# A decoder block's output projection as seven block products instead of eight

## The chip, the cores and the metric

One core of a Trainium2 chip runs the kernel. The time is device microseconds of one execution, as the median of several runs. The core has five engines that run side by side, each through its own instructions in order: TensorE (PE: matmuls; its weight loads, PEld, overlap them), VectorE (DVE), ScalarE (ACT), GpSimd (POOL) and SyncE (SP, which here only issues DMAs). An instruction waits on semaphores for what it reads, and everything behind it on its engine waits with it.

## The reference

One decoder block, all in float32, for 512 tokens of 1024 channels. What matters here is the middle:

```python
merged = (sigmoid(g_attn) * (attn @ w_branch_attn)
          + sigmoid(g_pool) * (pool @ w_branch_pool))   # 512 x 1024
x = x + gate1 * (merged @ w_out)                        # w_out 1024 x 1024
h2 = rms_norm(x, norm2_g) * (1 + scale2) + shift2
u = causal_dwconv(h2 @ w_up, conv_w, conv_b)            # w_up 1024 x 5632
x = x + gate2 * ((silu(u_g) * u_v) @ w_down)            # w_down 2816 x 1024
```

Ahead of it stand an RMS norm, the input projection, attention of 8 heads with a bias by distance, and a pooling branch. The six vectors shift1, scale1, gate1, shift2, scale2, gate2 are `silu(c) @ ada_w + ada_b`, cut in six parts (numbered 0 to 5 in the kernel).

## The kernel before

**Number format.** TensorE multiplies in a reduced format (float32r). Each operand is therefore split into a high part (a copy, `_h` or `hi_`, on ACT) and a low part (operand minus high part, `_l` or `lo_`, on DVE or POOL), and every product is three matmuls: high·high, high·low, low·high (`mm3`, `more`, lines 133 to 135 and 139 to 141). A matmul contracts 128 rows and writes 128 x 512 float32, one PSUM bank. There are eight banks.

**Stages, in order of time.** Input projections P, Q, K, V (up to about 106 us); eight attention heads with the gate projections between them (106 to 226); eight blocks j of the branch projections (226 to 270); the output projection with residual and second norm (270 to 323); the up projection (315 to 550, its convolution to 555); the down projection (550 to the end). The last two are done already as products of sums of blocks: the eight products of 2 x 2 blocks are replaced by seven, of sums `s1` to `s4` on one side and `t1` to `t4` on the other. For the down projection the weights' sums are made by POOL's DMAs: `t_step` loads a block, adds another with an adding DMA, stores the sum to DRAM (`tsum`), and SP loads it again later. No two steps of one tile follow each other without waiting for the DMA to land.

**Order.** The schedule is written by hand: each engine does its instructions in the order in which the Python code issues them.

**Names.** `plan` lists the weight units that SP loads, `ahead(name, n)` loads and splits n units beyond the named one. `ada_col(g, k)` loads a 512 KB block and sums it on DVE (line 207, `raw_ada`) into one column of `acol`: block k of vector g. `row_of(g)` turns eight columns into a row across all partitions by three DMAs of POOL (`g_d`, `g`). `bias_rows(h)` issues POOL's DMA of head h's bias (`trev`), which line 603 adds to the logits. In the branch loop, `gate` tiles become the merged block j (channels 128 j on the partitions, 512 tokens along), `mg_h` and `mg_l` are its parts, and the eight 1024-wide blocks of w_out (`raw_wo`) are split by ACT and POOL (`wo_h`, `wo_l`). Then `out_mm(t, f, ..)` makes 128 tokens t of half f of the channels: 8 k x 3 matmuls into a bank `o`. `out_post` multiplies by gate1 (`g`) and adds to `x`; `out_norm` squares and sums (ACT and DVE), takes the power -1/2 on POOL (`rs_y`), scales (`xn`) and stores x to DRAM (`x2d`). `flip_h2` transposes `xn` on TensorE (`hT`), and ACT and DVE make `h2f`, `h2h`, `h2l`, which the up projection reads (`u`). In the down stage `b` are blocks of w_down, `a` and `s` blocks and sums of the activations, X, Y, Z the accumulating banks.

**Where the ada sums stood.** Of the eight blocks of vector 5 (gate2), six are summed in the Q, K and V stages, block 6 in the output projection, block 7 behind the second transposes. Of vector 4 (scale2), blocks 0 and 1 are summed in heads 6 and 7, and six blocks in the output projection.

## Time and profile before

| | |
|---|---|
| three runs, us | 661.79, 661.38, 661.92 (median 661.79) |
| profiled execution, us | 661.57, its span 659.8, granted clock 0.998 |
| output projection on TensorE | 270.16 to 315.49 us |
| second transposes on TensorE | 321.24 to 322.91 us |
| ada sums on DVE | 48, 60.6 us in all, mean 1277 ns |
| weights from HBM, whole span | 120.90 MB read, 15.76 MB written |

The profile is one execution of the program. It has busy times by engine, the chain of work that ended last, groups of instructions by line and tile, and rows of a timeline. A row of the timeline reads: start in us, duration in us, engine, line, operation, written tile, operands and shape, number of instructions, and in brackets how long the engine stood idle before it and for whom. DMA rows by tile end with the size and the median time from issue to landing in us.

### The profile page before, as it was taken

Reading aid. Unit: us, or ns where it says so; the run is one execution under the profiler, and the core shown is the slowest. Engines: PE = TensorE matmul, PEld = TensorE weight load, DVE = VectorE, ACT = ScalarE, POOL = GpSimd, SP = SyncE. Lnnn points to the kernel's source line nnn. Section 1 sums busy time; section 2 is a strip of 40 time slices with the busy share of each in tenths; the row PEclk is TensorE's granted clock in tenths of the full one; section 3 lists DMA queues with packets and bytes.
Section 4 is the critical chain, followed back from the end, with each engine's and each line's share of the span. In section 5 each row is a group of like instructions: output and inputs, shape, how many; then the busy total and the mean of one; then the engine's idle time right before and its main releaser. Section 6 shows DMA issues by size and latency. Waiting matters only on the chain.

```text
span 659.8 us, 9672 instructions
## 1 busy us (share of the span) xinstructions
PE 652.9 (99%) x3493; PEld 562.8 (85%) x3493; DVE 546.5 (83%) x932; ACT 374.0 (57%) x651; POOL 146.2 (22%) x195
## 2 busy tenths in 40 slices
PE   8999999999999999999999999999999999999997
PEld 6788788888888888888998899998999988888886
DVE  6997897788878878847679799998999797878774
ACT  8555346756664566403756566665756655768431
POOL 3003050000000046613434444444532000000000
PEclk9999999999999999999999999999999999999999
DMA  8897353255552686764599999999996343655761
GB/s 347 317 311 271 98 191 113 69 183 184 171 176 97 214 193 223 234 254 153 169 206 239 272 257 275 258 308 275 266 268 227 118 143 95 231 190 187 270 216 55
DMA packets 43365, 137.29 MB, mean 208 GB/s; under 512 B 5699, under 2 KB 6380, under 8 KB 43318
## 3 DMA queue, kind: packets, MB, share of 16 engines
q1 hardware_dynamic: 28646, 98.23, 43.7%
q0 software_dynamic: 14672, 38.45, 22.9%
q8 instruction: 27, 0.44, 0.3%
q14 instruction: 20, 0.16, 0.1%
HBM read 120.90 MB, written 15.76 MB: 207 GB/s over the span
## 4 chain that ended last, share of the span: by engine, by line
PE 96%; DMA 1%; DVE 1%; SPq 0%; ACT 0%; issue 0%
PE u L133 7%; PE u L134 7%; PE u L135 7%; PE gate_ps L133 4%; PE gate_ps L134 4%; PE gate_ps L135 4%; PE X L140 3%; PE X L139 3%; PE X L141 3%; PE uX L139 3%; PE uX L141 3%; PE uX L140 3%; PE o L135 2%; PE o L133 2%; PE o L134 2%; PE q L149 2%
## 5 line engine op out<-in xcount | busy, mean ns | idle before, releaser
L133 PE MATMUL u<-h2h,hi_up 128*128 128x512 f32 (+1 forms) x224 | 80.5, 359 | 0.0
L134 PE MATMUL u<-h2l,hi_up 128*128 128x512 f32 (+1 forms) x224 | 80.4, 359 | 0.0
L135 PE MATMUL u<-h2h,lo_up 128*128 128x512 f32 (+1 forms) x224 | 80.4, 359 | 0.0
L207 DVE CUSTOM_DVE_ANT_0 raw_ada<-raw_ada,cbc,pk 128x1024 f32<-128x1024 f32 x48 | 60.6, 1277 | 0.0
L133 PE MATMUL gate_ps<-h_h,hi_gate 128*128 128x512 f32 x128 | 50.1, 391 | 0.0
L134 PE MATMUL gate_ps<-h_l,hi_gate 128*128 128x512 f32 x128 | 50.0, 390 | 0.0
L135 PE MATMUL gate_ps<-h_h,lo_gate 128*128 128x512 f32 x128 | 50.0, 390 | 0.0
L135 PEld LDWEIGHTS u<-h2h,lo_up 128*128 128x128 f32 x224 | 42.3, 189 | 6.3
L133 PEld LDWEIGHTS u<-h2h,hi_up 128*128 128x128 f32 x224 | 42.3, 189 | 6.0
L134 PEld LDWEIGHTS u<-h2l,hi_up 128*128 128x128 f32 x224 | 42.3, 189 | 6.0
L765 POOL DMA_DIRECT2D ta<-in_wdn x33 | 29.5, 900 | 26.8 <-DMA tsum_t<-ta 17.8
L124 DVE TENSOR_TENSOR lo_t<-raw_t,hi_t 128x1024 fp32r<-128x1024 f32 (+1 forms) x24 | 26.6, 1130 | 8.9 <-ACT hi_t L114 8.9
L114 ACT ACTIVATE hi_t<-raw_t 128x1024 fp32r<-128x1024 f32 (+1 forms) x24 | 23.7, 987 | 17.2 <-PE Y L141 8.1
L766 POOL DMA_DIRECT2D tsum_t<-ta x33 | 18.5, 560 | 52.9 <-DMA ta<-in_wdn 51.1
L607 ACT ACTIVATE L<-L,mn 128x512 f32<-128x512 f32 (+3 forms) x32 | 17.6, 552 | 20.1 <-DVE mn L603 20.1
L135 PEld LDWEIGHTS gate_ps<-h_h,lo_gate 128*128 128x128 f32 x128 | 24.0, 188 | 5.1
L133 PEld LDWEIGHTS gate_ps<-h_h,hi_gate 128*128 128x128 f32 x128 | 24.0, 188 | 4.8 <-DVE mn L603 0.3
L220 POOL TENSOR_TENSOR wo_l<-raw_wo,wo_h 128x512 fp32r<-128x512 f32 x16 | 24.0, 1521 | 18.1 <-ACT wo_h L219 18.1
L134 PEld LDWEIGHTS gate_ps<-h_l,hi_gate 128*128 128x128 f32 x128 | 24.0, 188 | 4.5
L114 ACT ACTIVATE hi_up<-raw_up 128x1024 fp32r<-128x1024 f32 x24 | 25.0, 1049 | 4.3 <-PE u L134 4.3
L1250 POOL DMA_DIRECT2D x2r<-x2d x8 | 4.6, 574 | 93.5 <-DVE dt L1243 88.8
L133 PE MATMUL o<-wo_h,mg_h 128*128 128x512 f32 x64 | 25.0, 391 | 0.0
(357 smaller groups left out, 2114.7 us busy)
## 6 DMA issues: line engine op xcount, KB each, us to landing
raw_ada<-in_ada SPq DMA_DIRECT2D x48, 512.0 KB, 5.0
raw_up<-in_wup SPq DMA_DIRECT2D x44, 512.0 KB, 5.8
ta<-in_wdn POOLq DMA_DIRECT2D x44, 256.0 KB, 6.4
raw_t<-tsum_t SPq DMA_DIRECT2D x20, 512.0 KB, 3.9
tsum_t<-ta POOLq DMA_DIRECT2D x33, 256.0 KB, 5.0
raw_gate<-in_wch SPq DMA_DIRECT2D x16, 512.0 KB, 4.0
raw_b<-in_wdn SPq DMA_DIRECT2D x15, 512.0 KB, 4.2
tc<-in_wdn POOLq DMA_DIRECT2D x22, 256.0 KB, 6.2
```

The costliest lines, as they stand in the source:

```text
L114: nc.scalar.activation(hi, raw, AF.Copy)
L124: nc.vector.tensor_sub(lo, raw, hi.bitcast(F32))
L133: nc.tensor.matmul(ps, sh, mh, start=start, stop=False)
L134: nc.tensor.matmul(ps, sh, ml, start=False, stop=False)
L135: nc.tensor.matmul(ps, sl, mh, start=False, stop=stop)
L139: nc.tensor.matmul(ps, sh, mh, start=start, stop=False, skip_group_check=True)
L140: nc.tensor.matmul(ps, sh, ml, start=False, stop=False, skip_group_check=True)
L141: nc.tensor.matmul(ps, sl, mh, start=False, stop=stop, skip_group_check=True)
L207: nc.vector.tensor_tensor_reduce(out=raw, in0=raw, in1=cbc, op0=ALU.mult, op1=ALU.add, scale=1.0, scalar=col(C_AB + i), accum_out=acol[:, ...
L220: (eng or nc.vector).tensor_sub(lo[:, :w], src, hi[:, :w].bitcast(F32))
L765: add = lambda to, nm: nc.gpsimd.dma_start(to, wdn[plain[nm], i][:, us], accum_op=ALU.add)
L766: store = lambda nm, t: nc.gpsimd.dma_start(tsum[nm, i][:, us], t)
```

## The change

The output projection becomes seven products of 2 x 2 blocks. On the side of the merged activations (a11: channels 0 to 511 of tokens 0 to 255, a12: channels 512 to 1023 of the same tokens; a21 and a22 the same for tokens 256 to 511) DVE makes four sums of blocks, `gs1` to `gs4`. On the side of the weights (512 x 512 blocks b11, b12, b21, b22) POOL's DMAs make t1 to t4 during the attention heads (`out_sums`, by the same `t_step`) and store them to DRAM (`osum`). The products are a11·b11 (into banks X), a12·b21 (Z), s1·t1 (Y), s2·t2 (X), s4·b22 (Y), s3·t3 (X), a22·t4 (X), 24 matmuls of 128 x 512 each; X goes on accumulating through four of them, and ACT copies a bank's state out where it is needed in between (`ok`). The rest of the diff:

- The loop over the branch blocks splits `br` units up to two ahead and not beyond the last; the first two up units are split in the output projection.
- The low parts of b11, b21, t1, t2 are made by POOL, of b22 and t4 by DVE. Those of t3 go another way: ACT copies the high part and negates the raw block in place, four adding DMAs of POOL add the high part to it, ACT negates the result (`o_high`, `o_low`).
- The reads of banks X after s3·t3 (`o_add(2 + p, 1, "X", ..)`) stand ahead of the norms of tokens 0 to 255. a22·t4 goes into the same banks.
- `bias_rows` is issued three heads ahead instead of two.
- Vector 4's blocks 0 to 5 are summed where vector 5's were (Q, K and V stages) and 6 and 7 in the last heads. Vector 5's eight: one in the up loop behind unit 3, three before the last convolution of the up stage, one in the first product of the down stage, three in the second.

The core of the diff:

```diff
-        def t_step(kk, n):
+        def t_step(kk, n, src, dst, hold):
...
+        def out_sums(h):
+            for n in range(h % 4 * 2, h % 4 * 2 + 2):
+                for kk in range(h // 4 * 2, h // 4 * 2 + 2):
+                    if n < 7:
+                        t_step(kk, n, osrc, osum, bias[0])
...
-            if h + 2 < H:
-                bias_rows(h + 2)
+            if h + 3 < H:
+                bias_rows(h + 3)
+            out_sums(h)
...
+        def o_high(nm):
+            res = []
+            for i in range(2):
+                raw = load_unit(osrc(nm, i), f"wo_{nm}_{i}")
+                for s in range(2):
+                    hi = slot(f"wo_{nm}_{2 * i + s}_h", F32R)
+                    nc.scalar.activation(hi, raw[:, s * 512 : s * 512 + 512], AF.Copy)
+                    res.append((hi, raw[:, s * 512 : s * 512 + 512]))
+                nc.scalar.activation(raw, raw, AF.Copy, scale=-1.0)
+            for hi, r in res:
+                nc.gpsimd.dma_start(r, hi.bitcast(F32), accum_op=ALU.add)
+            return res
+        def o_low(nm, res):
+            for k, (hi, r) in enumerate(res):
+                lo = slot(f"wo_{nm}_{k}_l", F32R)
+                nc.scalar.activation(lo, r, AF.Copy, scale=-1.0)
+                wo[nm, k] = hi, lo
+        o_prod("a11", "b11", "X", by_k=True)
+        o_fetch(0, 0)
+        g_sum("s1")
+        low()
+        g_hi("s1")
+        g_sum("s2")
+        g_lo("s1")
+        o_keep("s1", "X")
+        g_hi("s2")
+        g_sum("s3")
+        g_lo("s2")
+        g_sum("s4")
+        o_prod("a12", "b21", "Z", by_k=True)
+        g_hi("s4")
+        g_lo("s4")
+        for i in range(2):
+            o_split("b22", i)
+        o_prod("s1", "t1", "Y")
+        for p in range(2):
+            o_res(p, 0, o_add(p, 0, "Z", plus="s1"))
+        o_fetch(0, 1)
+        ahead("up0", 1)
+        o_keep("s5", "Y")
+        g_hi("s3")
+        g_lo("s3")
+        t3 = o_high("t3")
+        for p in range(2):
+            o_square(p, 0)
+        o_prod("s2", "t2", "X")
+        o_keep("s2", "X")
+        o_fetch(1, 1)
+        for i in range(2):
+            o_split("t4", i)
+        o_low("t3", t3)
+        o_prod("s4", "b22", "Y")
+        for p in range(2):
+            o_res(p, 1, o_add(p, 1, "Y", minus=(None, "s2")))
+            o_square(p, 1)
+        for p in range(2):
+            o_root(p)
+        o_fetch(1, 0)
+        o_prod("s3", "t3", "X")
+        tail = []
+        for p in range(2):
+            tail.append(o_add(2 + p, 1, "X", minus=("s5", None)))
+            o_norm(p)
+        o_prod("a22", "t4", "X", (0,), range(2))
+        tps = turn_h2(1)
+        o_prod("a22", "t4", "X", (0,), range(2, 4))
+        o_prod("a22", "t4", "X", (1,))
+        for p in range(2):
+            o_res(2 + p, 1, tail[p])
+        def first_half():
+            o_res(2, 0, oacc["X", 0], slot("ot_2_0"))
+        take_h2(1, tps, {3: first_half, 5: lambda: o_square(2, 1, True), 6: lambda: o_square(3, 1, True)})
+        o_res(3, 0, oacc["X", 1], slot("ot_3_0"))
+        for p in range(2):
+            o_square(2 + p, 0)
+            o_root(2 + p)
+        for p in range(2):
+            o_norm(2 + p)
...
+                if j == 3:
+                    ada_col(5, 0)
...
+        for k in range(1, 4):
+            ada_col(5, k)
         behind(0)
         behind(1)
```

How instructions stand at three places. First DVE behind the last block of the branch loop, where the output projection begins. Before (the three gate operations of the last block, the merged block's low part, then ada sums; `acol 128x1` reads the sum out):

```order
446 L853 TENSOR_TENSOR gate_2482<-gate_2482,B_2858 128x512
447 L854 TENSOR_TENSOR gate_1855<-gate_1855,A_2871 128x512
448 L855 TENSOR_TENSOR gate_2482<-gate_2482,gate_1855 128x512
449 L220 TENSOR_TENSOR mg_l<-gate_2482,mg_h 128x512
450 L207 ISA raw_ada_2901,acol<-raw_ada_2901,cbc,pk 128x1024
451 L207 ISA acol 128x1
```

Of the changed kernel, the same place (`gs` are the block sums; the gate tiles on the right are merged blocks):

```order
446 L884 TENSOR_TENSOR gate_2542<-gate_2542,gate_1893 128x512
447 L892 SCALAR_TENSOR_TENSOR acol<-acol,pk 128x8
448 L938 TENSOR_TENSOR gs_0_2991<-gate_1929,gate_2289 128x256
449 L938 TENSOR_TENSOR gs_0_2991<-gate_2073,gate_2418 128x256
450 L938 TENSOR_TENSOR gs_1_2994<-gate_2109,gate_2454 128x256
451 L938 TENSOR_TENSOR gs_1_2994<-gate_2256,gate_2542 128x256
452 L867 TENSOR_TENSOR mgl_2942<-gate_2542,mgh_2941 128x512
```

The ada sums have left the place, and the sums and low parts of the merged blocks follow the last gate addition directly.

Second POOL in the output projection of the changed kernel: fetches of x, stores of x2d, the four adding DMAs for t3 (`raw_wo_t`, line 1045) and the powers of the first two norms.

```order
103 L1045 DMA raw_wo_t_0_3152<-wo_t_0_h 128x512
104 L1045 DMA raw_wo_t_0_3152<-wo_t_1_h 128x512
105 L987 DMA x_2_1_3204<-in_x 128x512
106 L987 DMA x_3_1_3206<-in_x 128x512
107 L1045 DMA raw_wo_t_1_3159<-wo_t_2_h 128x512
108 L1045 DMA raw_wo_t_1_3159<-wo_t_3_h 128x512
109 L1032 DMA x2d_1_3316<-x_0_1_3124 128x512
110 L1032 DMA x2d_1_3326<-x_1_1_3126 128x512
111 L987 DMA x_2_0_3280<-in_x 128x512
112 L987 DMA x_3_0_3282<-in_x 128x512
113 L1024 TENSOR_TENSOR rs_y_3274<-ms_y_3272,mhalf 128x1
114 L1024 TENSOR_TENSOR rs_y_3278<-ms_y_3276,mhalf 128x1
```

Before, POOL had no adding DMA here, and each norm's power stood behind the stores of its own tokens. Now the powers of two norms stand behind all these rows.

Third DVE before the last convolution of the up stage (`ug`, `uv`: the two halves of the last unit, convolved by line 1131, 963 before). Of the changed kernel:

```order
838 L1176 TENSOR_TENSOR s_4_6084<-s_4_6084,a_4_5671 128x512
839 L1177 TENSOR_TENSOR a_4_5673<-a_4_5671,a_4_5673 128x512
840 L207 ISA raw_ada_6096,acol<-raw_ada_6096,cbc,pk 128x1024
842 L207 ISA raw_ada_6099,acol<-raw_ada_6099,cbc,pk 128x1024
844 L207 ISA raw_ada_6102,acol<-raw_ada_6102,cbc,pk 128x1024
846 L1131 SCALAR_TENSOR_TENSOR ug_6105<-u_6009,pk,ug_6105 128x511
847 L1131 SCALAR_TENSOR_TENSOR uv_6107<-u_6010,pk,uv_6107 128x511
```

The rows left out read the sums out (`acol 128x1`). Before, rows 819 and 820 (`a_4`, then `ug`) followed each other; three ada sums now stand between them.

More of the change, by code (lines that the diff above doesn't have):

```diff
@@ L786, in t_step @@
                 store("t4", tb.pop(kk)[0])
+        osum = {(n, i): dpool.tile([P, D], F32, name=f"osum_{n}_{i}") for n in ("t1", "t2", "t3", "t4") for i in range(2)}
+        oat = {"b11": 0, "b12": 1, "b21": 4, "b22": 5}
+        osrc = lambda nm, i: osum[nm, i] if nm[0] == "t" else wout[oat[nm] + 2 * i]
+        def out_sums(h):
[3 more added lines that the diff above has]
+                        t_step(kk, n, osrc, osum, bias[0])
         gates = {}
@@ new lines, in g_hi, with g_lo, g_of @@
+        def g_hi(nm):
+            for q in range(2):
+                hi = slot(f"g{nm}_{q}_h", F32R)
+                nc.scalar.activation(hi, gsum[nm, q], AF.Copy)
+                gform[nm, q] = hi, slot(f"g{nm}_{q}_l", F32R)
+        def g_lo(nm):
+            for q in range(2):
+                hi, lo = gform[nm, q]
+                nc.vector.tensor_sub(lo, gsum[nm, q], hi.bitcast(F32))
+        def g_of(nm, k, p):
+            if nm == "a11" or nm[0] == "s":
+                o = k % 2 * 256 + p * P
+                src = (ah[k // 2], al[k // 2]) if nm == "a11" else gform[nm, k // 2]
+            else:
+                o = (nm == "a22") * 256 + p * P
+                src = ah[k + 4], al[k + 4]
+            return [t[:, o : o + P] for t in src]
@@ new lines, in block_kernel, with o_prod @@
+        oacc, okept, ofresh = {}, {}, set()
+        def o_prod(an, bn, acc, ps=(0, 1), ks=range(4), by_k=False):
+            for p, k in ([(p, k) for k in ks for p in ps] if by_k else [(p, k) for p in ps for k in ks]):
+                if (acc, p) not in oacc:
+                    oacc[acc, p] = bank(f"o{acc}_{p}")
+                a, w = g_of(an, k, p), wo[bn, k]
+                more(oacc[acc, p], a[0], a[1], w[0], w[1], (acc, p) not in ofresh, k == 3)
+                ofresh.add((acc, p))
@@ L906, in out_post, with o_square @@
             nc.vector.tensor_mul(tmp, ps, g1[f])
-            between()
             nc.vector.tensor_add(xr[t, f], xr[t, f], tmp)
-        def out_norm(t):
-            row = [xr[t, 0], xr[t, 1]]
-            rs = rms_rows(row, f"y{t}")
-            rss[4 + t] = rs
+        osq = {}
+        def o_square(t, f, on_dve=False):
+            if t not in osq:
+                osq[t] = mini.tile([P, 2], F32, tag="ss", name=f"ss_y{t}")
+            junk = slot(f"junk_y{t}_{f}")
+            if on_dve:
+                nc.vector.tensor_tensor_reduce(
+                    out=junk, in0=xr[t, f], in1=xr[t, f], op0=ALU.mult, op1=ALU.add, scale=1.0 / D,
+                    scalar=0.0, accum_out=osq[t][:, f : f + 1])
+            else:
+                nc.scalar.activation(junk, xr[t, f], AF.Square, scale=1.0 / math.sqrt(D), accum_out=osq[t][:, f : f + 1])
@@ L917, in out_norm @@
                 xn2[t, f] = n_
                 x2d[t, f] = dpool.tile([P, 512], F32, name=f"x2d_{t}_{f}")
[L919 to L939 removed]
+                nc.gpsimd.dma_start(x2d[t, f], xr[t, f])
@@ L951, in block_kernel @@
+        for p in range(2):
+            o_norm(2 + p)
         fa, forms = {}, {}
```

149 lines of the change are left out of this document (90 added, 59 removed).

## The prediction

> **What bounds the kernel now.** I read the page's head first, then who TensorE waited for, then the stage of the output projection piece by piece.
>
> ```profile
> span 659.8 us, 9672 instructions
> PE 652.9 (99%) x3493; PEld 562.8 (85%) x3493; DVE 546.5 (83%) x932; ACT 374.0 (57%) x651; POOL 146.2 (22%) x195
> PEclk9999999999999999999999999999999999999999
> PE 96%; DMA 1%; DVE 1%; SPq 0%; ACT 0%; issue 0%
> ```
>
> ```profile
> PE xT L284 <- DVE wm L164: 1.5, 1, 1.5
> PE xT L298 <- ACT x L290: 0.9, 2, 0.5
> PE uX L139 <- ACT ka L1126: 0.4, 1, 0.4
> ```
>
> The second fence is all that TensorE waited for in the whole span: 2.8 us. TensorE is the bound from end to end and its clock is granted in full in every slice. So matmuls that go come off the time one for one, and every microsecond that TensorE must newly wait goes back on. DVE has 17% idle, ACT 43%; whether that idle time lies in the right place is the question here.
>
> ```profile
> L133 PE MATMUL o<-wo_h,mg_h 128*128 128x512 f32 x64 | 25.0, 391 | 0.0
> 270.16 0.39 PE L133 MATMUL o<-wo_h,mg_h 128*128 128x512 f32 x1
> 308.25 1.92 PE L880 MATMUL hT<-pk,xn 128*128 128x128 f32 x16
> 309.92 0.47 PE L133 MATMUL o<-wo_h,mg_h 128*128 128x512 f32 x1
> 315.49 0.28 PE L133 MATMUL u<-h2h,hi_up 128*128 128x256 f32 x1
> 315.60 0.28 PE L134 MATMUL u<-h2l,hi_up 128*128 128x256 f32 x1
> 322.91 0.37 PE L133 MATMUL u<-h2h,hi_up 128*128 128x256 f32 x1
> ```
>
> The projection is 64 matmuls on each of three lines (L133 to L135, one row quoted), 192 in all, from 270.16 to 315.49, with 16 transposes inside (308.25 to 309.92, 1.67 us). So one 512-wide matmul takes (45.33 - 1.67) / 192 = 0.227 us of the stream; the 391 ns in the group row is its pipelined duration, not its price. A 256-wide one steps by 0.12 us (315.49, then about 315.6).
>
> ```profile
> 227.00:275.00 48.00, 48.00 (x214) 39.72 (x213) 38.35 (x48) 32.61 (x52) 25.80 (x19) 1.00 0.74 213
> 275.00:321.00 46.00, 46.00 (x234) 39.24 (x233) 30.08 (x61) 11.77 (x26) 12.39 (x25) 1.00 0.55 194
> ```
>
> Columns: stretch, its length, busy time (and count) of PE, its weight loads, DVE, ACT, POOL, then clock, DMA share, GB/s. In 275 to 321 DVE has 15.9 us free and ACT 34.2. The change spends them.
>
> **TensorE's gain.** Seven products of 24 matmuls are 168, so 24 fewer: 24 x 0.227 = **5.45 us** off. [...]
>
> **What must be ready, and when.** I lay the new order on the old clock, products of 24 x 0.227 = 5.45 us from 270.16: a11·b11 to 275.6, a12·b21 to 281.05, s1·t1 to 286.5, s2·t2 to 291.9, s4·b22 to 297.4, s3·t3 to 302.8, then a22·t4 with the transposes of tokens 0 and 1 inside.
>
> ```profile
> 271.47 1.14 ACT L219 ACTIVATE wo_h<-raw_wo 128x512 fp32r<-128x512 f32 x2
> 269.48 1.04 ACT L114 ACTIVATE hi_up<-raw_up 128x1024 fp32r<-128x1024 f32 x1
> 273.01 1.00 DVE L855 TENSOR_TENSOR gate<-gate,gate 128x512 f32<-128x512 f32 x1
> 275.64 1.27 DVE L207 CUSTOM_DVE_ANT_0 raw_ada<-raw_ada,cbc,pk 128x1024 f32<-128x1024 f32 x1
> 288.04 0.69 DVE L906 TENSOR_TENSOR ot<-o,g 128x512 f32<-128x512 f32 x1 [7.51 <-PE o L135]
> 288.77 0.69 DVE L908 TENSOR_TENSOR x<-x,ot 128x512 f32<-128x512 f32 x1
> 310.87 0.76 DVE L890 TENSOR_TENSOR h2l<-h2f,h2h 128x256 fp32r<-128x256 f32 x2
> ```
>
> Prices: ACT copies of 512 about 0.55, of 1024 about 0.95 (1.04 less the overlap); DVE 512-wide 0.6 in a stream and 0.72 behind the one it needs (288.04 to 288.77); 256-wide 0.35 (half of 0.76, less overlap). Over the stage DVE gets 16 block sums (16 x 0.35), 16 low parts of sums, b22 and t4 (16 x 0.6) and six more adds that read a bank (6 x 0.65), 19.1 us, and loses seven ada sums of 1.27, 8.9: 10 more into 15.9 free. In order from the last gate add (273.01 + 1.00): s1 to 275.4, the low part of the last merged block 276.0, s2 277.4, s1's low parts 278.6, s3 280.0, s2's low parts 281.2, s4 282.6, its low parts 283.8, b22's 286.2. Wanted are s1 at 281.05, s2 at 286.5, s4 and b22 at 291.9. The first five products wait for nothing; the least lead is the 2.5 us of s1, and behind it each late microsecond would be one of TensorE's.
>
> **Term 1, the low parts of t3.** They go round by ACT, POOL and a DMA: ACT copies the high part and negates the block, POOL issues an adding DMA, ACT negates the sum.
>
> ```profile
> 327.17 0.91 POOL L765 DMA_DIRECT2D ta<-in_wdn  x1 [3.09 <-DMA ta<-in_wdn]
> 333.25 0.58 POOL L766 DMA_DIRECT2D tsum_t<-ta  x1 [1.19 <-DMA ta<-in_wdn]
> ta<-in_wdn POOLq DMA_DIRECT2D x44, 256.0 KB, 6.4
> g<-g_d POOLq DMA_DIRECT2D x4, 256.0 KB, 4.7
> g_d<-acol POOLq DMA_DIRECT2D x2, 4.0 KB, 13.5
> ```
>
> ACT begins when s1·t1 leaves its second bank (286.5): two copies out, two of s3, two of t3 (6 x 0.55), a negation (0.95) is 290.7; two more copies and a negation, 292.8. POOL issues two adds at 290.7 and 291.6 (0.91 each), fetches two pieces of x (0.6 each), and issues the last two at 293.7 and 294.6. The add issued at 327.17 let its store go at 333.25, so 6.1 us: the last two land at 299.8 and 300.7, and ACT's copies end at 300.4 and 301.3. TensorE wants the four low parts at 297.6, 298.3, 299.0 and 299.7: the third comes 1.4 late and the fourth, with the stream pushed back by that, 0.2 more. An add between two tiles of the chip's own memory isn't in this trace; by 4.7 us (a plain load) 0.2 is left, by 6.4 some 1.9. I take **+1.5**, by the adding row, which is the nearest (bounds 0.2 and 1.9).
>
> **Term 2, the first transposes.**
>
> ```profile
> 319.29 0.56 POOL L198 TENSOR_TENSOR rs_y<-ms_y,mhalf 128x1 f32<-128x1 f32 x1 [0.25 <-DVE ms_y L196]
> 319.88 0.89 DVE L916 TENSOR_SCALAR xn<-x,rs_y 128x512 f32<-128x512 f32 x2 [0.69 <-POOL rs_y L198]
> 300.13 1.22 POOL L898 DMA_DIRECT2D x<-in_x  x2
> ```
>
> The right half of x for tokens 0 and 1 (blocks of 128 rows) follows t4's low parts on DVE (about 297.5): 0.6 + 0.72 + 0.72 each, so 299.5 and 301.6. The squares stand on ACT behind t3's low parts, done by 302.9. On POOL the powers stand behind two stores of x2 and two fetches (1.22) and end near 304.0 and 304.6; then DVE has four scalings of 0.45 and a bank read (0.6) between them: xn of token 1 is there near 306.0. TensorE comes for it at 302.8 + 1.5 + six matmuls = 305.7: **+0.3** (bounds 0 and 1.0). The bank reads stand ahead of the norms, done by 303.7 when a22·t4 wants X at 304.3: free. Behind them they would end near 306.5, and cost 2.2.
>
> **Term 3, the turn into the up projection.**
>
> ```profile
> 316.00 0.42 ACT L889 ACTIVATE h2h<-h2f 128x256 fp32r<-128x256 f32 x1
> 316.32 0.61 ACT L190 ACTIVATE junk_y<-x 128x512 f32<-128x512 f32 x1
> 316.45 0.42 DVE L890 TENSOR_TENSOR h2l<-h2f,h2h 128x256 fp32r<-128x256 f32 x1 [0.54 <-ACT h2h L889]
> ```
>
> From the transposes (308.25) to the end of the last low part (316.87) are 8.6 us, at ACT's pitch. DVE's gaps of 0.5 between low parts must now hold a residual (1.4) and two squares (0.7 each): 2.8 into four gaps, of which 0.7 doesn't fit: 9.3. TensorE has behind the transposes' start these themselves (1.67), 18 matmuls (4.1) and 22 of the first up unit ahead of the one that reads the eighth low part (22 x 0.12 = 2.6): 8.4. By that 0.9; ACT has no bank to wait for in between, so I take **+0.7** (bounds 0.1 and 1.0). Before, 24 matmuls stood where 18 stand, and no ACT work came late.
>
> **Term 4, the second transposes.** From that last low part: the residual of token 3 (1.4), its square on ACT (0.61, taken as 0.8 with its sum read out), the sum and the power (0.25 + 0.56), and behind token 2's scaling its own (0.65): 3.7 us. TensorE has the unit's last two matmuls and the next 24: 3.1. **+0.6** (bounds 0 and 1.1).
>
> **Term 5, three ada sums ahead of the last convolution.**
>
> ```profile
> 551.64 0.75 DVE L963 SCALAR_TENSOR_TENSOR uv<-u,pk,uv 128x511 f32<-128x511 f32 x1 [2.56 <-ACT uv L959]
> 554.75 2.36 DVE L124 TENSOR_TENSOR lo_b<-raw_b,hi_b 128x1024 fp32r<-128x1024 f32 x2 [0.19 <-ACT hi_b L114]
> 556.29 0.39 PE L140 MATMUL X<-lo_b,a_h 128*128 128x512 f32 x1
> ```
>
> 3 x 1.21 = 3.6 us go into a wait of 2.56, so the convolution is 1.0 late, ACT's high part behind it too, and the low part that was there at about 556.0 for the matmul at 556.29 comes 0.7 after it: **+0.7** (bounds 0 and 1.0). The other late ada sums, one behind unit 3 of the up projection and four in the down products, have units split two ahead as cover: 0, or 1.2 for the first if DVE's lead is gone.
>
> **Moves at no cost.** The sums of weights are 40 DMAs of 256 KB on POOL's queue in the attention heads, in two chained steps a head.
>
> ```profile
> 105.00:175.00 70.00, 70.00 (x360) 59.34 (x359) 59.36 (x142) 46.55 (x100) 2.19 (x4) 1.00 0.43 140
> L603 DVE CUSTOM_DVE_ANT_0 L<-S,trev x32: 275/481/692, 107.4 to 212.8; 128x512 f32<-128x512 f32 x8, 128x384 f32<-128x384 f32 x8, 128x256 f32<-128x256 f32 x8, 128x128 f32<-128x128 f32 x8
> ```
>
> POOL does 2.2 us in 70 there and DMA stands at 0.43. A head lasts (212.8 - 107.4) / 7.4 or some 14 us; two chained steps of 6.4 are 12.8. A bias row now queued behind them is issued a head earlier than it was, so it lands ten or more microseconds ahead; each microsecond beyond that would stop DVE, then TensorE. POOL's splits of b11, b21, t1, t2 are as many as those of wo before. No cost.
>
> **Sum.** -5.45 + 1.5 + 0.3 + 0.7 + 0.6 + 0.7 = -1.65. The profiled execution took 661.57 us (span 659.8), 0.22 under the median of 661.79: **659.9 us**. With all lower bounds -5.15 (656.4), with all upper ones and the lone ada sum +1.75 (663.3).
>
> **Rivals.** **Full cover**: the adds land as plain loads and the norm chains run in each other's shadow, and 0.3 to 1.5 us is lost: 656.4 to 657.6, chance 0.12. For it, DVE and ACT have half the stage free on the mean; against it, four chains of rows with no slack. **Gain eaten**: ACT, without a gap from 286.5 to 302, sets the turn; one to three microseconds more there (t4's blocks land late, or its copies wait on DVE) push t3's low parts, the squares and so the powers: 660.5 to 663.1, chance 0.27. **Slower**: the adds of t3 wait at POOL or in the DMA engines. Terms 2 to 5 leave 3.15 us of gain, so 0.2% slower (663.1) needs a stall of 4.7 there: a landing after 9.3 us instead of 6.1. The 13.5 of the small write shows that POOL's DMAs can take so long, the 6.4 of 44 others speaks against it. If each of four adds waited out a DVE instruction of up to 1.27, the last would be 5 us later: 665, chance 0.11 with all else that ends slower. [...]
>
> [...]
>
> **Chances.** Forecast (657.6 to 660.5) 0.50, full cover 0.12, eaten 0.27, slower 0.11. A measurement can't tell a difference under 0.2% (1.3 us) from none: faster 0.62, same 0.27, slower 0.11. The range leaves out the best of full cover and most of slower: 656.9 to 662.9.
>
> **What would show it.** 168 matmuls into the o banks, 24 fewer on TensorE; waits of TensorE on t3's low parts (ACT), on xn twice and h2l once (DVE), on lo_b after unit 1 of the down products (DVE); the second transposes' end some 2.4 us ahead of 322.91 on the same clock; no wait of TensorE between 105 and 225. A wait of more than 4 us for t3, a wait for trev or for mg_l's product, or a granted clock under 1.00 would make it wrong.

## The result, and the profile after

| | before | after |
|---|---|---|
| median, us | 661.63 (4 runs, 661.38 to 661.92) | **668.02** (4 runs, 665.40 to 668.46) |
| ratio | | 1.0088, 95% interval 1.0062 to 1.0115 |
| profiled execution, us (span) | 661.57 (659.8) | 668.46 (666.7) |

The change makes the kernel 0.9% slower. The page of the changed kernel, its head, the granted clock in 40 slices, and the shares of the chain that ended last:

```profile
span 666.7 us, 9758 instructions
PE 653.1 (98%) x3469; PEld 560.2 (84%) x3469; DVE 564.1 (85%) x966; ACT 392.3 (59%) x687; POOL 180.7 (27%) x243
PEclk9999999999999999996999999999999999999999
PE 81%; DVE 7%; DMA 5%; ACT 4%; issue 2%; POOL 1%; SPq 0%; ACTq 0%; DVEq 0%; POOLq 0%
```

The 24 matmuls are gone (3493 to 3469), but TensorE's busy time is what it was (653.1 us for 652.9), and one slice of the clock fell to 0.6: the matmuls that were saved were paid for by slow ones. All that TensorE waited for (total, times, longest):

```profile
PE oX L140 <- ACT wo_t_l L1052: 5.8, 4, 2.9
PE xT L284 <- DVE wm L164: 1.5, 1, 1.5
PE X L140 <- DVE lo_t L124: 0.7, 1, 0.7
PE X L140 <- DVE lo_b L124: 0.6, 1, 0.6
PE hT L907 <- DVE xn L1029: 0.4, 1, 0.4
PE uX L139 <- ACT ka L1294: 0.4, 1, 0.4
PE xT L298 <- ACT x L290: 0.3, 1, 0.3
```

New are the first row (t3's low parts), lo_t and lo_b (the low parts of the down weights' sums and blocks) in the down projection, and 0.4 us for xn. TensorE's timeline, from the first product to the up projection's second half:

```profile
269.96 0.39 PE L139 MATMUL oX<-wo_b_h,mgh 128*128 128x512 f32 x1
297.16 0.39 PE L139 MATMUL oX<-wo_t_h,gs_h 128*128 128x512 f32 x1
300.63 0.53 PE L140 MATMUL oX<-wo_t_l,gs_h 128*128 128x512 f32 x1 [1.94 <-ACT wo_t_l L1052]
304.89 0.79 PE L140 MATMUL oX<-wo_t_l,gs_h 128*128 128x512 f32 x1 [2.87 <-ACT wo_t_l L1052]
312.46 0.39 PE L139 MATMUL oX<-wo_t_h,mgh 128*128 128x512 f32 x1
313.83 1.92 PE L907 MATMUL hT<-pk,xn 128*128 128x128 f32 x16
319.71 0.28 PE L133 MATMUL u<-h2h,hi_up 128*128 128x256 f32 x1
328.28 0.36 PE L133 MATMUL u<-h2h,hi_up 128*128 128x256 f32 x1
```

Up to 297.16 the stream runs as forecast: five products in 27.20 us (five times 5.45 is 27.25). Then s3·t3 takes 15.30 us (297.16 to 312.46) in place of 5.45: **9.85 us** more. Of these 5.8 are waits; nearly all the rest is in the clock. The stretches of 2 us there (columns as in the prediction: stretch, length, PE, weight loads, DVE, ACT, POOL, clock, DMA share, GB/s):

```profile
300.00:302.00 2.00, 1.37 (x3) 0.62 (x3) 1.93 (x4) 0.58 (x1) 0.58 (x1) 0.74 1.08 249
302.00:304.00 2.00, 0.02 (x1) 0.00 (x0) 0.28 (x1) 0.00 (x0) 1.42 (x3) 0.50 1.07 342
308.00:310.00 2.00, 2.00 (x6) 1.62 (x5) 1.60 (x5) 0.58 (x2) 1.15 (x2) 0.50 0.98 365
```

The clock falls to a half at about 301 (0.74 on the mean of 300 to 302), and in 308 to 310, with nothing to wait for, only six matmuls start where nine would. And the DMA share is 1.0 throughout. Before, in the same stretch, it was half of that:

```profile
302.00:304.00 2.00, 2.00 (x11) 1.65 (x10) 0.81 (x2) 0.09 (x1) 0.00 (x0) 1.00 0.54 209
```

What fills the DMA engines, and what it does to t3's adds: SP's five loads for the up projection, ACT waiting for the third add, and the adds as a group (size and median landing).

```profile
292.17 15.54 SPq L82 DMA_DIRECT2D raw_up<-in_wup  x5
304.21 0.63 ACT L1052 ACTIVATE wo_t_l<-raw_wo_t 128x512 fp32r<-128x512 f32 x1 [3.63 <-DMA raw_wo_t<-wo_t_h]
```

```profile
raw_wo_t<-wo_t_h POOLq DMA_DIRECT2D x4, 256.0 KB, 9.6
```

### The profile page after: what moved, and what is told of

It reads as the page before. It is cut to its first block, busy times and chain, and to the rows that moved or that the text cites. A ratio compares the mean times of both kernels' runs of the same rounds, so it can differ in the third digit from the quotient of the medians.

```text
span 666.7 us, 9758 instructions
## 1 busy us (share of the span) xinstructions
PE 653.1 (98%) x3469; PEld 560.2 (84%) x3469; DVE 564.1 (85%) x966; ACT 392.3 (59%) x687; POOL 180.7 (27%) x243
## 4 chain that ended last, share of the span: by engine, by line
PE 81%; DVE 7%; DMA 5%; ACT 4%; issue 2%; POOL 1%; SPq 0%; ACTq 0%; DVEq 0%; POOLq 0%
PE u L134 6%; PE u L135 6%; PE u L133 6%; PE gate_ps L133 4%; PE gate_ps L135 4%; PE gate_ps L134 4%; PE uX L139 3%; PE uX L141 3%; PE uX L140 3%; DMA raw_wo_t<-wo_t_h 2%; PE q L149 2%; PE p L149 2%; PE X L140 2%; DMA raw_b<-in_wdn 2%; PE X L141 2%
## 5 line engine op out<-in xcount | busy, mean ns | idle before, releaser
L841 POOL DMA_DIRECT2D g_d<-acol x2 | 1.8, 922 | 120.6 <-DVE acol L207 120.6
L607 ACT ACTIVATE L<-L,mn 128x512 f32<-128x512 f32 (+3 forms) x32 | 17.6, 552 | 19.9 <-DVE mn L603 19.9
L114 ACT ACTIVATE hi_b<-raw_b 128x1024 fp32r<-128x1024 f32 (+1 forms) x18 | 17.5, 983 | 16.3 <-PE X L141 4.9
L124 DVE TENSOR_TENSOR lo_b<-raw_b,hi_b 128x1024 fp32r<-128x1024 f32 (+1 forms) x18 | 19.9, 1129 | 6.0 <-ACT hi_b L114 6.0
```

The source lines that it names most:

```text
L114: nc.scalar.activation(hi, raw, AF.Copy)
L124: nc.vector.tensor_sub(lo, raw, hi.bitcast(F32))
```

## Experiments

All are compared with the kernel before on the same chip, whose median was 661.46 to 661.71 in each. A time is the median; a number behind it in brackets is the ratio, which goes by the means, with its 95% interval.

### 1. Why t3's low parts come late

Theory: the adds share the DMA engines with SP's loads; rivals: an add between two tiles is slow by itself, or the halved clock is the loss.

**t3 split like t4** (ACT the high part, DVE the low part), no adding DMA:

```diff
-        t3 = o_high("t3")
+        for i in range(2):
+            o_split("t3", i)
...
-        o_low("t3", t3)
```

> The low parts of t3 are made like those of t4: high part on ACT, subtraction on DVE; no negations, no adding DMAs. Theory (the adds of t3 are what makes the changed kernel slow): no wait of TensorE for t3, the granted clock 1.00 throughout, s3·t3 takes 5.45 us instead of the 15.3 of the changed kernel, of which some 0.6 comes back as a wait for xn ahead of the first transposes; 668.0 - 9.3 = 658.7 us, faster than before by 0.4%. Rival (the new sums on DVE and ACT are too many and the adds only hid that): DVE, with 2.4 us more, is late for t4 or the norms, TensorE waits 2 us or more there, 661 or above.

Measured 662.89 us (1.0025, 1.0014 to 1.0035): 5.1 of the 6.4 lost microseconds come back, and 4.2 stay out that I had expected. The wait for t3 is gone, and another stands in its place, the banks X not yet read out by DVE (`ot`). The clock, which I had expected full, falls here too, to 0.50 in 306 to 308 us, behind that wait:

```profile
PE oX L139 <- DVE ot L997: 2.4, 1, 2.4
```

**Four up loads held back** until ACT has the last of t3's low parts (a one-column write into their buffers, which reads that part):

```diff
         o_low("t3", t3)
+        for i in range(2, 6):
+            early[f"up{i}"] = wraw_p.tile([P, 1024], F32, tag="raw", name=f"raw_up{i}")
+            nc.scalar.activation(early[f"up{i}"][:, :1], wo["t3", 3][1][:, :1].bitcast(F32), AF.Copy)
+            nc.sync.dma_start(early[f"up{i}"], wup[i])
```

> The changed kernel, but four loads of up-projection weights (units 2 to 5) wait until ACT has the last low part of t3, so they no longer share the DMA engines with the adds. Theory queue (the adds are slow because SP's 512 KB loads fill the same DMA engines): the adds land in about 6 us, TensorE waits for them 1.5 us or less, the clock stays up, about 660 us. Theory own cost (an add between two tiles of the chip's memory is slow by itself): landing stays at 8 us or more, the waits at 4 or more, 666 us or above.

Measured 664.41 us (1.0041, 1.0026 to 1.0055), its ten runs from 660.86 to 667.13; the profiled one is the fastest. In it the adds land as I had priced them:

```profile
raw_wo_t<-wo_t_h POOLq DMA_DIRECT2D x4, 256.0 KB, 6.1
```

TensorE's wait for t3 is 1.7 us there and the clock stays at 1; the down projection starts 278.6 us behind the output projection, against 286.0 in the changed kernel and 280.4 before. So the loads make the adds late. The median is 3.5 us above that run. In eight of the ten runs the mean granted clock is 0.996 or 0.997, in the other two (660.86 and 663.20 us) 1.0, so in most of them the clock still falls for a while; the last run of section 3 shows such an execution.

**Seven transfers on an idle chip.** Behind the last output POOL issues transfers of 256 KB: an add from DRAM (the first row below), two adds between tiles and a plain copy between tiles (the last row), each waiting for the one before, then three adds between tiles at once.

```diff
+        dz = [t_tile(f"dz_{i}") for i in range(4)]
...
+        nc.gpsimd.dma_start(dz[0], wout[4][:, :512], accum_op=ALU.add)
+        nc.gpsimd.dma_start(dz[0], dz[1], accum_op=ALU.add)
+        nc.gpsimd.dma_start(dz[0], dz[2], accum_op=ALU.add)
+        nc.gpsimd.dma_start(dz[3], dz[0])
+        for i in range(1, 4):
+            nc.gpsimd.dma_start(dz[i], dz[0], accum_op=ALU.add)
```

> The changed kernel with seven DMAs of 256 KB more behind its last output, when nothing else runs: one add from DRAM, two adds between tiles one after the other, one plain copy between tiles, then three adds between tiles at once. Its time says nothing. Theory queue: an add between tiles lands alone in 3 to 5 us, near the plain copy and the add from DRAM, the three at once in less than 8. Theory own cost: alone it takes 6 or more and clearly longer than the copy, the three at once over 10.

```profile
668.55 0.88 POOL L1506 DMA_DIRECT2D dz<-in_wout  x1 [0.97 <-DMA dz<-in_wout]
673.60 0.87 POOL L1507 DMA_DIRECT2D dz<-dz  x1 [4.17 <-DMA dz<-in_wout]
677.15 0.85 POOL L1508 DMA_DIRECT2D dz<-dz  x1 [2.67 <-DMA dz<-dz]
680.73 0.57 POOL L1509 DMA_DIRECT2D dz<-dz  x1 [2.73 <-DMA dz<-dz]
```

From issue to issue an add from DRAM is 5.05 us and one between tiles 3.55 and 3.58. From issue to landing the add between tiles takes 3.3, the plain copy 2.3, and the three adds at once 3.5 in the median. The rival falls: the add the change uses is the cheaper one when nothing else moves.

**TensorE kept busy in the waits** by 27 matmuls into an unused bank:

```diff
+                if an == "s3" and p == 0:
+                    for _ in range((1, 9, 13, 4)[k]):
+                        nc.tensor.matmul(spare[0], wo["t2", 0][0][:, :P], wo["t2", 0][0], start=True, stop=True, skip_group_check=True)
```

> The changed kernel with 27 more matmuls of 128x512 into an unused bank (1, 9, 13 and 4 of them ahead of the four steps of s3·t3 that wait for low parts), so that TensorE works where it waited; their result is not used. Theory clock (the granted clock halves because TensorE idles): it stays at 1.00, the 14 matmuls behind the last wait take 0.227 instead of 0.43 us, some 2 us faster than the changed kernel in spite of 6 us more of work, about 666 us. Rival (the clock falls for another cause, or the waits alone make the loss): the same 668 or slower.

Measured 668.75 us (1.0101, 1.0084 to 1.0119), not the 666 expected. The clock stays at 1 in every slice, and at 0.999 or more in all four runs (0.992 to 0.997 in the changed kernel's), so it was the idling that halved it; but the up projection starts only 0.9 us earlier (318.8 for 319.7), since the fillers take the time that the half clock took, and the median shows no gain. The adds land after 9.5 us, as in the changed kernel. The clock is the smaller part of the loss; the adds set when s3·t3 can end.

### 2. The chain behind s3·t3

**Bank reads behind the norms**, on the first run's kernel:

```diff
         for p in range(2):
-            tail.append(o_add(2 + p, 1, "X", minus=("s5", None)))
             o_norm(p)
+        for p in range(2):
+            tail.append(o_add(2 + p, 1, "X", minus=("s5", None)))
```

> The run with t3 split by ACT and DVE (662.89 us), with the reads of banks X behind the norms instead of ahead of them. Theory (the reads end the wait ahead of a22*t4, which was 2.4 us in that run): four scalings of 0.69 us and the power on POOL come in front of them, the wait grows to 4.5 to 6 us, part of it comes back since the transposes find xn ready (0.6 us): 664.5 to 666 us. Rival (the end of the chain is xn and the turn into the up projection, not the banks): the time is the same within 0.5, 662.4 to 663.4.

Measured 666.24 us (1.0071, 1.0058 to 1.0083), 3.4 us slower than with the reads ahead; the wait for them grows from 2.4 to 4.3 us. This part of the change is right.

**A read ahead of the sums of squares too** (the read of the first bank X moved above `o_root`):

```diff
-        for p in range(2):
-            o_root(p)
         o_fetch(1, 0)
         o_prod("s3", "t3", "X")
         tail = []
         for p in range(2):
             tail.append(o_add(2 + p, 1, "X", minus=("s5", None)))
+            if p == 0:
+                for q in range(2):
+                    o_root(q)
             o_norm(p)
```

> As the kernel with t3 on DVE (e1), but DVE reads the first bank X after s3·t3 ahead of the two sums of squares it must wait for, instead of behind them. Theory (there TensorE's 2.4 us are spent behind a wait of DVE for ACT's squares): the wait at the first a22·t4 falls to 0.5 us or less, but the transposes then wait for xn of token 1, which is not earlier; 0.5 to 1.5 us faster than e1's 662.9. Rival (DVE itself is late, not its wait): no change.

Measured 662.90 us (1.0017, 1.0007 to 1.0026): no gain. TensorE still waits 2.1 us ahead of a22·t4 (2.4 without the edit), and its wait for xn grows from 0.6 to 2.2.

**The same, with t3's low parts by POOL**, and t4 loaded and split ahead of the first two up units (`early`, `his`: loaded and copied first, their low parts behind `o_root`):

```diff
-            o_split("t3", i)
+            o_split("t3", i, nc.gpsimd)
...
             o_split("t4", i)
+        for i in range(2):
+            early[f"up{i}"] = load_unit(wup[i], f"up{i}")
+            his[f"up{i}"] = hi_of(f"up{i}", early[f"up{i}"])
```

> t3's low parts by POOL's subtraction, t4 split ahead of the first two up units, whose low parts go behind the bank read, and the bank read ahead of the sums of squares. Theory (the products are fine, and only the order of the work around s3·t3 and the adds lost the gain): no wait of TensorE of more than 1 us from 270 to 323, the up projection begins 3 us earlier than before, 658.5 us, 0.45% faster than before. Rival (the stage has too little room on DVE and ACT): waits of 2 us or more remain, 661 or above.

Measured 662.89 us (1.0023, 1.0014 to 1.0033): no gain again. TensorE waits 2.3 us for xn and 1.1 for ms_y (the mean square that the power is taken of). Why, section 4 shows.

### 3. The late gate2 sums

**The kernel before with only the moved sums** of vectors 4 and 5 and the row of gate2 (all places as in the change; the first and the last of them):

```diff
-        ada_col(5, 4)
-        ada_col(5, 5)
+        ada_col(4, 0)
+        ada_col(4, 1)
...
+                    if i in (1, 3, 5):
+                        ada_col(5, 5 + i // 2)
...
                 keep("s5", "Y")
+                g2 = row_of(5, "g2")
```

> The kernel before with this part of the change alone: the ada sums of scale2 moved ahead, those of gate2 late (one in the up loop, three ahead of the last convolution, four in the down products, and gate2's row after the second of these). Theory: a wait for lo_b of 0.6 us at the second unit of the down stage, and in some executions a wait for lo_t near the end of the fifth product, since the 4-byte pieces of gate2's row now go through the DMA engines among weights; raw_b then lands after 8 us or more instead of 3. 662.4 us, up to 663. Rival (these moves cost nothing): 661.6.

Measured 664.45 us (1.0039, 1.0027 to 1.0051): **2.9 us**, of which I had forecast 0.7. In its profile 0.7 of them are there before the branch stage's first `A` product (230.1 for 229.4), 0.9 at lo_b, and the rest at lo_t. The 0.7 is not shown to come from the moves: the first Q product already starts that much later (17.6 for 16.9), and in runs that share everything up to there, such as the changed kernel and those derived from it, it starts anywhere from 16.7 to 17.6. Two rows of the changed kernel's timeline, POOL's write of the row and ACT's wait behind it, point to where lo_t's lateness comes from:

```profile
587.83 0.92 POOL L841 DMA_DIRECT2D g_d<-acol  x1 [75.15 <-DVE acol L207]
601.51 1.06 ACT L114 ACTIVATE hi_b<-raw_b 128x1024 fp32r<-128x1024 f32 x1 [4.79 <-DMA raw_b<-in_wdn]
```

**The row out of the way**: that kernel, with the row made from gate1's columns at the end of the up stage; it leaves out gate2's own row:

```diff
         behind(0)
         behind(1)
+        g2 = row_of(2, "g2")
...
-                g2 = row_of(5, "g2")
```

> The kernel before with the change's places for the ada sums of vectors 4 and 5, as in the run that had only these moves (664.45 us), but gate2's row is made from gate1's columns at the end of the up stage, so that its write in small pieces lies no longer among the down stage's weight loads; the output is scaled by gate1 in place of gate2. Theory (the row's write delays the loads, raw_b lands after 10 us in place of 3): the wait for lo_t (1.0 us) goes, 1.3 us come back, 663.2 us, between 662.8 and 663.6. Rival (the late sums themselves, six more 512 KB loads and 1.3 us of DVE each, make the weights late): 664.4 as before this edit, lo_t late by about 1 us still.

Measured 663.83 us (1.0029, 1.0018 to 1.0039), 0.6 back in the median where I had expected 1.3; in the profiled run, the fastest of seven, the wait for lo_t is gone. So the row is a part of the 2.9 us, and by the median the smaller one; the 0.6 at lo_b stays. The loads of the down weights from 576 to 604 us, with the late row and then without:

```profile
raw_b<-in_wdn SPq DMA_DIRECT2D x5, 512.0 KB, 11.3
g_d<-acol POOLq DMA_DIRECT2D x1, 4.0 KB, 12.2
```

```profile
raw_b<-in_wdn SPq DMA_DIRECT2D x5, 512.0 KB, 4.4
```

With the write of eight columns (4 KB, by line 841's pattern in 4-byte pieces) among them, the 512 KB loads take more than twice as long to land: 11.3 us for 4.4. The same pair on the fastest version (section 5) shows 10.4 us with the late row and 3.3 without.

**Sums ahead of the last convolution**: the kernel with t3's low parts by POOL, one of its three sums there moved into the first down product:

```diff
-        for k in range(1, 4):
+        for k in range(1, 3):
             ada_col(5, k)
...
-                    if i == NU - 1:
-                        ada_col(5, 4)
+                    if i >= NU - 2:
+                        ada_col(5, 3 + i - (NU - 2))
```

> As e6, but two ada sums instead of three stand ahead of the last convolution, and the third is made at the end of the first product of the down stage. Theory (term 5: 3.6 us go into a wait of 2.56): TensorE's wait for lo_b of 0.6 goes, 0.7 us faster than e6, 657.8. Rival: lo_b is late for another reason and the wait stays.

Measured 661.99 us (1.0007, 0.9998 to 1.0015): 0.9 less, and lo_b's wait is gone.

**All eight spread over the up loop**, behind units with plain products, the row at the loop's end, and x fetched behind the first norms on POOL:

```diff
+        SPREAD = (3, 4, 7, 10, 12, 15, 18, 20)
...
-                if j == 3:
-                    ada_col(5, 0)
+                if j in SPREAD:
+                    ada_col(5, SPREAD.index(j))
...
+        g2 = row_of(5, "g2")
         s_forms(NU - 2)
```

> The run with the reordered chain and the earlier ada sums (661.99 us), with gate2's eight sums spread over the up loop behind the units that have two plain products (3, 4, 7, 10, 12, 15, 18, 20), its row issued at the end of that loop, and the fetch of x behind the first norms on POOL. Theory (row among the loads, and POOL's fetches ahead of the power, are what is left): no wait for lo_b or lo_t, xn earlier by 0.8 us, 660.3 us, between 659.5 and 661.2, which is below the kernel before. Rival (DVE has no room in the up loop, 27 to 29.5 of 30 us busy): waits for weights' low parts in the up loop, 662.5 to 665 us.

Measured 661.76 us (0.9999, 0.9990 to 1.0008), with no wait in the down stage: that loss is gone, but less is won than expected.

**The change itself, loads held and sums spread** (both edits as above):

> The change with four up loads held until t3's low parts are made (664.41 us, its runs from 660.86 to 667.13), and gate2's sums spread over the up loop with the row at its end. Theory (the adding DMAs among the up loads, and the late gate2 sums with their row, are the whole loss of the change): the waits for lo_b and lo_t go, 2.9 us by the run that had the moves alone: 661.5 us, between 660 and 662.5, with a narrower spread. Rival (the spread of the runs comes from the adding DMAs, which stay): the runs keep a spread of 4 us or more, median 662.5 to 664.

Measured 662.11 us (1.0010, 0.9999 to 1.0021), from 660.76 to 664.68. The two make up 5.9 of the change's 6.4 us. The spread stays, so it isn't the late sums'. It goes with the clock: the six runs whose mean granted clock is 1.0 took 660.76 to 661.69 us, the six with 0.997 took 662.54 to 664.68. The profiled one is of the second kind. Its adds land a little later than 6.1, TensorE waits 2.5 us for t3, at most 2.2 at once, and the clock halves behind that:

```profile
raw_wo_t<-wo_t_h POOLq DMA_DIRECT2D x4, 256.0 KB, 6.8
304.00:306.00 2.00, 2.00 (x6) 1.53 (x5) 1.43 (x5) 0.75 (x4) 1.57 (x3) 0.50 0.85 289
```

### 4. Where TensorE's gain went

Starts behind that of the output projection, from the first and last starts of the groups `o`, `u`, `hT`, `X` in each profiled execution:

| run | up projection starts | last of the second transposes | down projection starts |
|---|---|---|---|
| before | 45.3 | 52.7 | 280.4 |
| after | 49.7 | 58.3 | 286.0 |
| t3 by DVE (first run) | 44.3 | 52.7 | 280.4 |
| sums spread, t3 by POOL | 43.2 | 52.5 | 280.8 |
| POOL's low parts of up units (below) | 46.5 | 54.7 | 283.0 |
| sums spread, t3 by DVE (below) | **40.4** | **49.7** | **278.0** |

An up projection that starts earlier is worth nothing while its second half can't: the second transposes are the gate.

**Two low parts of up units from DVE to POOL**, to shorten DVE's chain to those transposes, and from behind the bank read to ahead of s4·b22:

```diff
-                nc.vector.tensor_sub(lo, raw, hi.bitcast(F32))
+                (nc.gpsimd if nm in ("up0", "up1") else nc.vector).tensor_sub(lo, raw, hi.bitcast(F32))
...
+        ahead("up0", 1)
         o_prod("s4", "b22", "Y")
...
-                ahead("up0", 0)
...
-        ahead("up1", 0)
```

> The run with the reordered chain and gate2's sums spread over the up loop (661.76 us), with the low parts of the first two up units made by POOL, idle there, in place of DVE. Theory (DVE's chain of bank reads, residuals, norms and h2l sets the end of the second transposes, and so the time): its 2.4 us less on DVE bring the second transposes from 52.5 to about 50.3 us behind the start of the output projection, and the time to 659.5 us, between 658.7 and 660.3, below the kernel before (661.56). Rival (the loads set it, or the chain's end is PE's own): the second transposes move by less than 0.7 us, 661.1 to 662 us; or POOL's low parts, 2.5 us each, push its power and stores back, and it is slower, 662 to 663.5 us.

Measured 665.73 us (1.0050, 1.0034 to 1.0066): 4 us slower than without, with a wait of TensorE for ms_y of 4.4 us (1.3 without). The edit moves engine and place at once; POOL's and DVE's rows of that run show what it does:

```profile
290.55 5.04 POOL L220 TENSOR_TENSOR wo_t_l<-raw_wo_t,wo_t_h 128x512 fp32r<-128x512 f32 x4
296.64 5.22 POOL L124 TENSOR_TENSOR lo_up<-raw_up,hi_up 128x1024 fp32r<-128x1024 f32 x2
```

```profile
289.61 6.53 DVE L955 TENSOR_TENSOR gs_l<-gs,gs_h 128x512 fp32r<-128x512 f32 x2
296.67 6.34 DVE L220 TENSOR_TENSOR wo_t_l<-raw_wo_t,wo_t_h 128x512 fp32r<-128x512 f32 x3
```

Two, and then three, subtractions of 0.68 us on DVE last 6.5 and 6.3 us. Without POOL beside them they would take some 1.3 and 1.9, so they are longer by 5.2 and 4.4, nearly the length of POOL's run (5.0 and 5.2). The reordered runs had lost 5 us of DVE in the same place: in each of the three one gs_l takes 5.9 us.

**t3's low parts back to DVE**, all else as in the run with the sums spread:

```diff
-            o_split("t3", i, nc.gpsimd)
+            o_split("t3", i)
```

> The run with the reordered chain and gate2's sums spread over the up loop (661.76 us), with t3's four low parts by DVE in place of POOL. Theory (while POOL subtracts two tiles, DVE's subtractions stand still): DVE gets four subtractions of 0.68 us, 2.7 us, and loses 5.2 us in which gs_l stood still, so its chain is 2.5 us shorter; the two gs_l take 1.3 us in place of 6.5, the wait for ms_y (1.3 us) goes, the second transposes end 50 to 51 us behind the start of the output projection in place of 52.5, and the time is 659.6 us, between 658.8 and 660.5, below the kernel before. Rival (the 6.5 us of gs_l are something else, a wait for ACT's high parts or a profile's artefact): DVE has 2.7 us more to do, the wait ahead of a22*t4 grows to about 4 us, 663 to 665 us.

Measured **658.68 us** (0.9952, 0.9938 to 0.9965): faster than both kernels. (0.4 of the 3.1 us lie outside the core's span, which is 659.6 and 656.9 us in the two median runs.) First DVE's and POOL's rows without the edit, then the same rows of DVE with it:

```profile
290.85 6.55 DVE L955 TENSOR_TENSOR gs_l<-gs,gs_h 128x512 fp32r<-128x512 f32 x2
291.45 5.95 DVE L955 TENSOR_TENSOR gs_l<-gs,gs_h 128x512 fp32r<-128x512 f32 x1
291.79 5.05 POOL L220 TENSOR_TENSOR wo_t_l<-raw_wo_t,wo_t_h 128x512 fp32r<-128x512 f32 x4
```

```profile
290.93 1.29 DVE L955 TENSOR_TENSOR gs_l<-gs,gs_h 128x512 fp32r<-128x512 f32 x2
292.13 4.90 DVE L220 TENSOR_TENSOR wo_t_l<-raw_wo_t,wo_t_h 128x512 fp32r<-128x512 f32 x8
```

6.55 us became 1.29, and the second transposes end 3.0 us earlier than before the change. The clock is full in all slices.

### 5. The other edits on the fastest version

**Bias rows two heads ahead again**, first on the kernel with t3 by DVE, then on the fastest:

```diff
-            if h + 3 < H:
-                bias_rows(h + 3)
+            if h + 2 < H:
+                bias_rows(h + 2)
```

> The run with t3 split by ACT and DVE (662.89 us), with the bias rows again two heads ahead. Theory of the prediction (this edit is worth nothing, the row lands long before its use either way): 662.9 us, within 0.5, no wait of TensorE between 106 and 226 us. Rival (the sums' DMAs on POOL hold the rows up, so that two heads are too few): a wait for trev or for the logits in the heads, 0.5 to 3 us more, 663.4 to 666.

> The fastest version (658.68 us) with the bias rows two heads ahead again. Theory (DVE waits for a head's bias row, 1.9 us once, and the heads get 0.6 us longer; the rest of the 2.9 us came from other places): 659.3 us, between 659.0 and 660.0, from the last K product to the first branch product 22.5 us in place of 22.2. Rival (it costs as much as there): 661 to 662 us. Rival of the prediction (nothing): 658.7.

Measured 665.75 us (1.0065, 1.0052 to 1.0077; 662.89 without), and 663.21 us (1.0009, 0.9993 to 1.0025; 658.68 without), here in two groups: five runs from 659.5 to 661.0, seven from 663.0 to 664.7. In the first of the two, DVE waits once for a bias row, which it didn't with three heads of lead:

```profile
DVE L L603 <- DMA trev<-fd: 1.9, 1, 1.9
```

In the profiled run of the second, one of the upper group (663.60), POOL and DVE stand so:

```profile
173.50 0.56 POOL L766 DMA_DIRECT2D osum_t<-ta  x1 [6.78 <-DMA ta<-in_wout]
176.13 0.87 POOL L765 DMA_DIRECT2D ta<-in_wout  x1 [2.07 <-DVE at_l L220]
176.70 0.86 POOL L580 DMA_DIRECT2D trev<-fd  x1
```

```profile
184.34 0.69 DVE L603 CUSTOM_DVE_ANT_0 L<-S,trev 128x512 f32<-128x512 f32 x1 [2.29 <-PE gate_ps L135]
```

A bias row waits on POOL behind a store and an add that wait for transfers to land, is issued at 176.70, and with the 6.5 us that such a row takes (median there) lands at 183.2 or later; DVE reads it at 184.34. (The row names TensorE as the releaser; of several semaphores the profile names one.) From the first product of the logits to the first `A` product of the branch stage are 129.4 us (104.6 to 234.0), and 125.3 in the fastest version (104.5 to 229.8); TensorE waits 2.7 us in this stretch, and not at all there. In the first of the two the stretch is only 0.6 us longer (125.9 for 125.3), so the rest of its 2.9 us isn't the heads'. So the sums of weights do hold the bias rows up, and the third head of lead pays for that, with 0.6 and 4.1 us in the two profiled executions; the lower group of runs shows that it isn't always as much.

**The change's places of gate2's sums**, on the fastest version (the edits of section 3 reversed):

> The fastest version (658.68 us) with gate2's sums and row where the change has them. Theory (three sums ahead of the last convolution make lo_b late, and the row among the down stage's loads makes lo_t late): 661.0 us, between 660.3 and 661.8, with waits for lo_b (0.6) and lo_t (0.6 to 1.3). Rival (as my prediction had it, 0.7 us and nothing in the down stage): 659.4.

Measured 660.69 us (0.9986, 0.9978 to 0.9995), 2.0 more than the fastest, with waits for lo_b (0.5) and lo_t (0.7).

## Why the prediction was wrong

I forecast 659.9 us and faster; it is 668.0 and slower, above the range. The rival that named the place, t3's adds waiting in the DMA engines, was the one that came true, with a chance of 0.11; the 663.1 to 665 us that I worked out for it were too low as well. The 665 took each add to wait out a DVE instruction, and no run shows that: from 296 to 302 us DVE is as busy with four loads held back as without (5.86 of 6 us in both), and the adds land after a median of 6.1 us with them held and 9.6 without.

- **TensorE's gain of 5.45**: right. The five products ahead of t3 ran at the forecast pace, to within 0.1 us.
- **Term 1 is the step that failed.** "The add issued at 327.17 let its store go at 333.25, so 6.1 us", with bounds of 0.2 and 1.9. The adds were issued when I said (from 291.0), but landed after a median of 9.6 us and at most 12.9. I priced the add by its kind and not by its place: I never counted the five 512 KB loads that SP issues from 292.17 on, as the buffers come free. With four of them held back the adds took 6.1 and 6.8 in two profiled runs, with the loads among them 9.5 and 8.1 in two others. The rival's point, "a landing after 9.3 us instead of 6.1", was well placed. The term also lacked the halved clock. Together +9.85 instead of +1.5.
- **Term 2**, +0.3: 0 here, since the longer stall gave xn time. In the runs without the stall DVE's chain cost TensorE 2.4 us (ot) or, where POOL stood in DVE's way, 2.7 (ms_y 1.3, xn 1.4) up to the first transposes; in the fastest version it is 0.3. "The bank reads ahead of the norms" are worth 3.4 us where I worked out 2.2; "free" they were not, since DVE comes to them late.
- **Terms 3 and 4**, together +1.3: the second half of the up projection starts 5.37 us later than before (328.28 for 322.91). With the start 0.2 us earlier, that is -5.45 + 9.85 + 1.2. Right in size here; in the fastest version, where no stall comes first, the same turn loses 1.9.
- **Term 5**, +0.7: 0.8 between the starts of the down stage's second product and the up stage's second half (571.8 for 565.6, less 5.37). Right.
- **The other late sums at 0**: wrong. The start of the last Y product (632.6 for 625.4) is 1.0 us later than the second product's: the row's write makes the weights late. I had costed the row's columns but not its DMA. Moved alone, sums and row cost 2.9 us in the median, and 2.2 in the profiled run from the first Q product on.
- **"Moves at no cost"** in the heads: the result is right, no wait of TensorE there. The reason was too easy: it holds only by the third head of lead: with two heads the kernels are 2.9 and 4.5 us slower, of which 0.6 and 4.1 lie in the heads.

The sum, made again from the measured terms: -0.2 - 5.45 + 9.85 + 1.2 + 0.8 + 1.0 = +7.2; the spans differ by 6.9.

The idea of seven products is good: 5.1 us came back with t3 split by DVE, 2.2 by the order behind it, 2.0 by spreading the sums, 9.3 in all, and 3.0 of the 5.45 stay as a gain. By the table of section 4 the fastest version loses 0.55 of the 5.45 before its up projection starts, which is 4.9 us earlier than before, 1.9 by the second transposes and 0.6 more by the start of the down projection. That leaves 2.4, the difference of the spans (659.8 and 657.4; its profiled run is the slowest of its five). TensorE's waits there for xn and h2l are 0.7 and 0.6; what else holds the second transposes isn't settled.

## What to carry to other kernels

Price a DMA by what else will be in the engines when it is issued, loads that the change itself lets go included; a landing time from a quieter stretch is no bound (6.1 us there, 9.6 here). Before moving elementwise work from a full DVE to an idle POOL, look at whether DVE's two-input rows stretch beside it: 10.3 us of POOL cost DVE 9.6 in one of these runs. And a tiny write in 4-byte pieces (loads beside it landed after 11.3 us, 4.4 without), or a row behind chained DMAs on one queue (4.1 us in the heads with two heads of lead), belongs where nothing waits for the transfers around it.

## What the hardware showed that I had not expected

- **DVE's two-input subtractions stood still beside POOL's**: 6.55 us for two on DVE beside four on POOL, 1.29 without. One of the two took 5.95 us around POOL's four in a row (5.05); its row starts 0.34 us before POOL's first. What holds DVE isn't shown, and it isn't so for every pair of rows: in the branch loop of the kernel before, an addition of two gate tiles on DVE took 0.99 us inside two of POOL's subtractions.

```profile
251.77 3.00 POOL L220 TENSOR_TENSOR wo_l<-raw_wo,wo_h 128x512 fp32r<-128x512 f32 x2 [2.11 <-ACT wo_h L219]
252.62 0.99 DVE L855 TENSOR_TENSOR gate<-gate,gate 128x512 f32<-128x512 f32 x1
```

- **The clock halved after short waits, though not always.** In the changed kernel the longest single wait up to 302 us had been 1.94 us, and the granted clock of 300 to 302 was already 0.74, then 0.50 up to 310. In the reordered run with one sum moved, three waits of 0.5, 0.9 and 1.1 us brought it to 0.57 in 308 to 312; in the run with the read ahead of the sums of squares, waits of 2.1, 0.8 and 1.1 us in the same place left it at 1.00. So neither the longest wait nor their sum decides alone, and what does stays open; two microseconds were not safe here.
- An adding DMA of 256 KB between tiles takes 3.6 us from issue to issue on an idle chip, less than one from DRAM (5.05), and 9.6 from issue to landing among 512 KB loads.
